# Reading x again and saving the bias: two transfers put at other places among the latent weights of layer 0

## The chip, the core and the metric

The kernel runs on one core of one Trainium2 chip. The metric is the device time of one execution in microseconds. Each kernel is run several times and the median is compared. Engines are called by the profile's short names: PE is TensorE (matmul), PEld its weight loads, DVE is VectorE, ACT is ScalarE, POOL is GpSimd, SP is SyncE, which here only issues transfers.

## The reference

A two-layer bidirectional encoder on 256 tokens of width 2048, all in float32. Each layer has an attention part with two groups of heads side by side, then an MLP of width 8192, and both parts are modulated by a conditioning vector `c`. Cut to what matters:

```python
mod = silu(c) @ w_ada[l] + b_ada[l]          # 6 vectors of 2048 per layer
h = rmsnorm(x) * (1 + sc_a) + sh_a
proj = h @ w_in[l]                           # dq, dk, dv, cq (512), ckv (256), kr (64)
out_a = diff_attention(dq, dk, dv, positions, bias_table, ...)     # 4 heads, two score maps each
q  = rmsnorm(cq,  q_norm_g[l])  @ w_uq[l]    # 8 heads x (128 plain + 64 positional)
kv = rmsnorm(ckv, kv_norm_g[l]) @ w_ukv[l]   # 8 heads x (128 keys + 128 values)
out_b = mla_attention(q_nope, rope(q_rope), k_nope, rope(kr), v_m)
x = x + g_a * (concat(out_a, out_b) @ w_o[l])
x = x + g_m * (relu(h2 @ w_mlp_in[l])**2 @ w_mlp_out[l])           # h2: x normed and modulated again
```

The result is the normed x after both layers.

## The kernel before

**How the work is tiled.** Activations stand transposed, 128 features by 256 tokens in a tile, and weights are streamed through the chip once. A weight tile comes as 128 partitions by 2048 float32 (1 MiB). For the large products the kernel splits each float32 number into a rounded part `hi` and a rest `lo` (`part`, lines 146 to 157): ScalarE copies the raw half tile into `hi` (line 151), VectorE subtracts to get `lo` (line 154), and TensorE makes three products per pair, hi with the activation's hi (line 194), hi with its lo (line 197) and lo with its hi (line 198); for value weights these are lines 296 to 298. So before TensorE can use a weight, it must have landed, ScalarE must have rounded both halves, and VectorE must have subtracted twice.

**Buffers.** Raw weight tiles rotate through five buffers named `raw`, the `hi` and `lo` halves through four each. The conditioning weights `w_ada` (`ada_load`, `ada_sums`) use the same five raw buffers: VectorE multiplies each such tile by the conditioning vector and sums it (line 380). About one conditioning tile is loaded per weight tile, by a running credit (`more_ada`), so the two streams alternate on SyncE. A transfer is issued when VectorE has freed its buffer.

**What sets the order.** The program is written in one sequence (`layer`, from line 867 on). A scheduler then lists the instructions for each engine, in an order that follows the written one and its own estimate of when inputs are ready; each of ScalarE, VectorE and SyncE works off its list strictly in order. `behind` pins one instruction after another. There is no hand-written table: where a transfer is written changes the scheduler's estimate, and with it the lists of all engines.

**The place.** After the keys of the differential heads come, in the order in which they are written:

- `up_k` (weights `w_uk`, one tile): the latent keys, eight tiles `pss`, copied as `kn`
- `probs(3)`: scores `psc` of the last differential head (line 1249), score minima (1251), exponentials on ScalarE (1236), and the combination on VectorE (1257, 1260, 1261)
- a copy of the attention bias to DRAM (line 981, `bias_kept`), since its buffer is later overwritten by the gate rows and layer 1 needs it again, and a second reading of the input x in token-major form (line 983, two transfers of 1 MiB into `self.xr`), which the residual updates need much later (lines 1117 and 1119). Both happen in layer 0 alone
- `up_q(0)`: plain queries of heads 0 to 3 (weights `w_uq[0, 0]`, 48 matmuls), copied as `qn`
- `turn(0)`: four transposes `pt` of the first head's probabilities (line 1268), copied as `aT` by ScalarE
- `up_r`: positional queries (weights `w_uq[0, 2]`, 48 matmuls), copied as `qr`, then rotated: a permutation matmul `pqr` (line 1222) and VectorE's lines 1225 to 1227
- `turn(1)`, the scores of the first latent head (`psm`, lines 1318 and 1319), `up_v`: the latent values (weights `w_uv`, `pv`, copied as `vm`)
- `turn(2)`, two more steps of latent heads, `up_q(1)`: plain queries of heads 4 to 7 (weights `w_uq[0, 1]`), and then the value projection with the remaining latent heads in between, and the output projection with the residual updates

All copies out of PSUM named here are line 346 on ScalarE.

Of the kernel before, what the change touches and what calls it, by code (L numbers as in the profile page):

```python
# [101 lines left out]
class Trunk:  # L102
# [764 lines left out]
    def layer(self, l, acc=None):  # L867
        nc, io = self.nc, self.io
# [52 lines left out]
        def up_q(b):  # L921
            qn.extend(self.copy(ps, "qn", ms) for ps in self.small(io["w_uq"][l, b], cq, 4))

        def up_r():
            raw = [self.copy(ps, "qr", ms) for ps in self.small(io["w_uq"][l, 2], cq, 4)]
            qr.extend(self.rope_q(x) for x in raw)

        def up_v():
            w = self.weights(io["w_uv"][l])
            for cg in range(2):  # L930
                pss = [self.bank("pv") for _ in range(2)]
                self.tokens_by_k(pss, [[z[:, 512 * cg : 512 * cg + 512] for z in y] for y in w], ckv, True, True)
                vm.append([self.copy(ps, "vm") for ps in pss])
# [12 lines left out]
        def probs(hd):  # L946
            return lambda: a.append(self.diff_probs(l, hd, q[hd], kk[hd]))

        def turn(hd):
            return lambda: at.append(self.transposed(a[hd]))  # L950
# [26 lines left out]
            self.rate = RATE_A2  # L977
        up_k()
        probs(3)()
        if l == 0:  # L980
            nc.sync.dma_start(self.bias_kept, self.row)
            for t in range(2):
                nc.sync.dma_start(self.xr[:, t], io["x"][t])
        up_q(0)
        turn(0)()
        up_r()
        turn(1)()
        mla[0]()
        up_v()
        turn(2)()  # L990
        for f in mla[1:3]:
            f()
# [441 lines left out]
```

## Time and profile before

| What | us |
|---|---|
| median of 3 runs | 2174.59 |
| lowest and highest | 2174.57, 2177.94 |
| the profiled execution: its own time | 2174.76 |
| its span, first to last instruction | 2172.8 |
| TensorE busy | 2144.7 |
| VectorE busy | 1590.9 |
| ScalarE busy | 1139.8 |

Times in rows of the profile count from the start of the span. In the order of time a row gives start, duration, engine, line, operation, tile written and tiles read, shape, count, and in brackets the idle time of the engine before it with what ended it. The groups of waits give the waiting line, the one that it waited for, total, times and the longest. In the stretches, the granted clock is the share of TensorE's full clock, and the DMA share is the mean busy share of the core's 16 DMA engines.

### The profile page before, as it was taken

How to read it: one execution, taken by the hardware profiler on the slowest of the kernel's cores; microseconds unless marked ns; L12 is line 12 of the kernel's file. 1: busy time of each engine (PE TensorE's matmuls, PEld its weight loads, DVE VectorE, ACT ScalarE, POOL GpSimd, SP SyncE). 2: the span in 40 equal slices, each digit the busy share in tenths (PEclk: the TensorE clock that was granted, in tenths of full speed). 3: DMA queues.
4: the chain of work that ended last, by engine and by line, in shares of the span. 5: the costliest groups of instructions: out<-in, count | busy, mean ns of one | idle time of the engine just before them, and what ended most of it. 6: DMA issues, size and time to landing. Idle time of an engine off the chain costs nothing.

```text
span 2172.8 us, 29358 instructions
## 1 busy us (share of the span) xinstructions
PE 2144.7 (99%) x11502; PEld 1863.5 (86%) x11502; DVE 1590.9 (73%) x2117; ACT 1139.8 (52%) x1725; POOL 6.8 (0%) x19
## 2 busy tenths in 40 slices
PE   7999999999999999999999999999999999999998
PEld 6899888898888888888889998888888888888886
DVE  7888888988688988888876876678555555555555
ACT  6555663565455355355454565556535534644643
POOL 0000000000000000000000000000000000000000
PEclk8999999999999999999999999999999999999999
DMA  9988889799888988888967766767655555565552
GB/s 387 423 340 330 320 328 357 290 330 344 314 329 326 352 315 320 321 333 320 336 224 278 253 229 224 290 214 273 233 199 182 200 194 177 192 208 179 194 195 96
DMA packets 87243, 594.76 MB, mean 274 GB/s; under 512 B 9856, under 2 KB 10304, under 8 KB 20288
## 3 DMA queue, kind: packets, MB, share of 16 engines
q1 hardware_dynamic: 85968, 587.08, 73.5%
q0 software_dynamic: 848, 5.28, 0.6%
q8 instruction: 90, 1.47, 0.3%
q10 hardware_dynamic: 288, 0.52, 0.1%
q14 instruction: 49, 0.40, 0.1%
HBM read 589.66 MB, written 3.18 MB: 273 GB/s over the span
## 4 chain that ended last, share of the span: by engine, by line
PE 97%; DVE 2%; DMA 1%; ACT 0%; SPq 0%; issue 0%; ACTq 0%
PE ps L217 19%; PE pr L312 13%; PE pr L311 13%; PE pr L314 13%; PE ps L220 10%; PE pk L260 3%; PE pk L284 2%; PE pk L194 2%; PE pk L198 2%; PE pk L197 2%; PE pv L298 2%; PE pv L296 2%; PE pv L297 2%; PE pk L281 1%; PE ps L198 1%; PE ps L197 1%
## 5 line engine op out<-in xcount | busy, mean ns | idle before, releaser
L154 DVE TENSOR_TENSOR lo<-raw,hi 128x1024 fp32r<-128x1024 f32 (+1 forms) x714 | 836.0, 1194 | 446.2 <-issue 215.5
L151 ACT ACTIVATE hi<-raw 128x1024 fp32r<-128x1024 f32 (+1 forms) x714 | 732.5, 1036 | 694.0 <-PE pr L312 375.9
L380 DVE SCALAR_TENSOR_TENSOR ada<-ada,cond 128x2048 f32<-128x2048 f32 x192 | 438.0, 2285 | 12.0 <-DMA ada<-in_w_ada 11.4
L217 PE MATMUL ps<-h,hi 128*128 128x512 f32 x1856 | 431.5, 390 | 0.0
L217 PEld LDWEIGHTS ps<-h,hi 128*128 128x128 f32 x1856 | 345.2, 188 | 69.4
L311 PE MATMUL pr<-hi,hid 128*128 128x512 f32 x1024 | 398.6, 389 | 0.0
L312 PE MATMUL pr<-hi,hid 128*128 128x512 f32 x1024 | 398.5, 389 | 0.0
L314 PE MATMUL pr<-lo,hid 128*128 128x512 f32 x1024 | 253.5, 389 | 0.0
L220 PEld LDWEIGHTS ps<-h,lo 128*128 128x128 f32 x1856 | 230.3, 192 | 4.5
L220 PE MATMUL ps<-h,lo 128*128 128x256 f32 x1856 | 231.7, 283 | 0.0
L314 PEld LDWEIGHTS pr<-lo,hid 128*128 128x128 f32 x1024 | 192.2, 188 | 39.9
L312 PEld LDWEIGHTS pr<-hi,hid 128*128 128x128 f32 x1024 | 192.3, 188 | 39.7
L311 PEld LDWEIGHTS pr<-hi,hid 128*128 128x128 f32 x1024 | 192.2, 188 | 39.6
L1192 ACT ACTIVATE sum<-ps 128x256 f32<-128x256 f32 x110 | 42.1, 382 | 117.8 <-PE ps L220 117.7
L194 PE MATMUL pk<-h,hi 128*128 128x256 f32 x320 | 90.5, 285 | 0.2 <-ACT h L705 0.2
L198 PE MATMUL pk<-h,lo 128*128 128x256 f32 x320 | 90.5, 283 | 0.0
L197 PE MATMUL pk<-h,hi 128*128 128x256 f32 x320 | 90.5, 283 | 0.0
L260 PE MATMUL pk<-hf,w 128*128 128x256 f32 x384 | 84.1, 379 | 0.5 <-ACT hf L677 0.5
L188 DVE TENSOR_TENSOR hid<-relu,hid 128x256 fp32r<-128x256 f32 x128 | 48.3, 421 | 49.5 <-ACT hid L187 49.5
L260 PEld LDWEIGHTS pk<-hf,w 128*128 128x128 f32 x384 | 72.7, 190 | 10.7 <-ACT hf L677 0.9
L194 PEld LDWEIGHTS pk<-h,hi 128*128 128x128 f32 x320 | 61.1, 192 | 0.6 <-ACT h L705 0.5
L198 PEld LDWEIGHTS pk<-h,lo 128*128 128x128 f32 x320 | 61.3, 192 | 0.2 <-DVE lo L154 0.2
(237 smaller groups left out, 2456.1 us busy)
## 6 DMA issues: line engine op xcount, KB each, us to landing
raw<-in_w_m SPq DMA_DIRECT2D x238, 1024.0 KB, 5.2
ada<-in_w_ada SPq DMA_DIRECT2D x192, 1024.0 KB, 6.5
raw<-in_w_o SPq DMA_DIRECT2D x32, 1024.0 KB, 6.0
raw<-in_w_m SPq DMA_DIRECT2D x24, 768.0 KB, 5.7
raw<-in_w_dv SPq DMA_DIRECT2D x16, 1024.0 KB, 5.5
raw<-in_w_t SPq DMA_DIRECT2D x12, 1024.0 KB, 5.2
w<-in_w_a SPq DMA_DIRECT2D x24, 384.0 KB, 13.5
raw<-in_w_a SPq DMA_DIRECT2D x12, 768.0 KB, 5.4
```

Source lines behind the costliest of these rows:

```text
L151: ins = self.nc.scalar.activation(hi, v, AF.Copy)
L154: ins = self.nc.vector.tensor_tensor(lo, v, hi.bitcast(F32), ALU.subtract)
L194: ins = mm(ps, hi, x[0], start=first, stop=False, skip_group_check=shared)
L197: mm(ps, hi, x[1], start=False, stop=False, skip_group_check=shared)
L198: self.last_mac = mm(ps, lo, x[0], start=False, stop=last, skip_group_check=shared)
L217: mm(ps.rearrange("p a b -> p (a b)"), part(w, k, 0), x[2], start=k == 0, stop=False)
L220: mm(ps[:, 0], part(w, k, 1), x[0], start=False, stop=k == nk - 1)
L260: self.nc.tensor.matmul(ps, v, whole[k], start=first, stop=last, skip_group_check=True)
L311: mm(ps, xh[:, c], part(i, 0), start=kq == 0 and i == 0, stop=False)
L312: mm(ps, xl[:, c], part(i, 0), start=False, stop=False)
L314: self.last_mm = mm(ps, xh[:, c], part(i, 1), start=False, stop=kq == 3 and i == 3)
L380: ins = nc.vector.scalar_tensor_tensor(w, w, 1.0, self.cond, ALU.mult, ALU.mult, accum_out=acc[:, i : i + 1])
```

## The change

The bias copy and the first half of the second reading of x are written after `up_r`, that is behind the loads of the first plain queries' and the positional queries' weights. The second half of x is written after `up_v`, behind the load of the latent values' weights. Before, all three were written ahead of `up_q(0)`. Nothing else is edited; what is computed stays the same.

```diff
         up_k()
         probs(3)()
-        if l == 0:
-            nc.sync.dma_start(self.bias_kept, self.row)
-            for t in range(2):
-                nc.sync.dma_start(self.xr[:, t], io["x"][t])
         up_q(0)
         turn(0)()
         up_r()
+        if l == 0:
+            nc.sync.dma_start(self.bias_kept, self.row)
+            nc.sync.dma_start(self.xr[:, 0], io["x"][0])
         turn(1)()
         mla[0]()
         up_v()
+        if l == 0:
+            nc.sync.dma_start(self.xr[:, 1], io["x"][1])
         turn(2)()
```

Lines below the edit stand one further down in the changed kernel (1236 becomes 1237, and so on), and some tiles have other numbers.

SyncE's list at the moved reads, from the conditioning tile behind `w_uk` on (ada is a tile of conditioning weights, raw a tile of weights; w_uq comes three times, for the first plain, the positional and the remaining plain queries). Before:

```order
L364 DMA ada_1833<-in_w_ada 128x2048
L983 DMA x<-in_x 128x2048 x2
L170 DMA raw_1929<-in_w_uq 128x2048
L364 DMA ada_1940<-in_w_ada 128x2048
L364 DMA ada_1942<-in_w_ada 128x2048
L170 DMA raw_2005<-in_w_uq 128x2048
L364 DMA ada_2018<-in_w_ada 128x2048
L170 DMA raw_2109<-in_w_uv 128x2048
L364 DMA ada_2121<-in_w_ada 128x2048
L170 DMA raw_2189<-in_w_uq 128x2048
```

And in the changed kernel:

```order
L364 DMA ada_1833<-in_w_ada 128x2048
L170 DMA raw_1926<-in_w_uq 128x2048
L364 DMA ada_1937<-in_w_ada 128x2048
L364 DMA ada_1939<-in_w_ada 128x2048
L170 DMA raw_2002<-in_w_uq 128x2048
L364 DMA ada_2015<-in_w_ada 128x2048
L985 DMA x<-in_x 128x2048
L170 DMA raw_2108<-in_w_uv 128x2048
L364 DMA ada_2120<-in_w_ada 128x2048
L990 DMA x<-in_x 128x2048
L170 DMA raw_2189<-in_w_uq 128x2048
```

The two reads of x went behind five and seven other transfers. The bias copy does not show here: the scheduler puts it further up, between two tiles of `w_t`, and it stands there in both kernels.

ScalarE's list at the latent queries (kn, k, qn, qr are copies of products; s are the exponentials of the last differential head; aT is the copy of transposed probabilities; hi is a rounded half of the raw tile named). Before:

```order
L346 ACTIVATE kn_1893<-pss_1880 128x512
L151 ACTIVATE hi_1931<-raw_1929 128x1024
L1236 ACTIVATE s_1896,tot_1902<-s_1896,mx_1897 128x256 x2
L151 ACTIVATE hi_1935<-raw_1929 128x1024
L1236 ACTIVATE s_1908,tot_1914<-s_1908,mx_1909 128x256 x2
L346 ACTIVATE qn_1969<-pss_1944 128x512
L346 ACTIVATE qn_1996<-pss_1971 128x512
L346 ACTIVATE aT_2003<-pt_1998 128x512
L151 ACTIVATE hi_2007<-raw_2005 128x1024
L151 ACTIVATE hi_2011<-raw_2005 128x1024
L346 ACTIVATE qr_2045<-pss_2020 128x512
```

And in the changed kernel, from the last exponentials of the head before on:

```order
L1237 ACTIVATE s_1740,tot_1746<-s_1740,mx_1741 128x256 x2
L151 ACTIVATE hi_1928<-raw_1926 128x1024
L151 ACTIVATE hi_1932<-raw_1926 128x1024
L346 ACTIVATE k_1819<-ps_1664 128x512
L346 ACTIVATE kn_1848<-pss_1835 128x512
L346 ACTIVATE kn_1863<-pss_1850 128x512
L346 ACTIVATE kn_1878<-pss_1865 128x512
L346 ACTIVATE kn_1893<-pss_1880 128x512
L1237 ACTIVATE s_1896,tot_1902<-s_1896,mx_1897 128x256 x2
L1237 ACTIVATE s_1908,tot_1914<-s_1908,mx_1909 128x256 x2
L151 ACTIVATE hi_2004<-raw_2002 128x1024
L151 ACTIVATE hi_2008<-raw_2002 128x1024
```

The rounds of the first queries' weights moved ahead of the last key's copy and of the four latent key copies, and those of the positional queries' weights moved ahead of the query copies. On VectorE the rests of the first queries' weights moved up too, ahead of the combination of the head before, and one conditioning sum (of ada_1833) moved ahead of the last head's score minima; it had stood behind them.

ScalarE's list further on, at the latent values (vm are copies of value tiles, sm the exponentials or the scaling of a latent head, raw_2189 the weights of the remaining plain queries). Before:

```order
L346 ACTIVATE aT_2091<-pt_2086 128x512
L151 ACTIVATE hi_2191<-raw_2189 128x1024
L151 ACTIVATE hi_2195<-raw_2189 128x1024
L1236 ACTIVATE sm_2094,tot_2102<-sm_2094,mxm_2095 128x256 x2
L346 ACTIVATE vm_2137<-pv_2123 128x512
L346 ACTIVATE vm_2139<-pv_2124 128x512
L346 ACTIVATE vm_2155<-pv_2141 128x512
L1324 ACTIVATE sm_2094<-sm_2094,r_2103 128x256 x2
L346 ACTIVATE vm_2157<-pv_2142 128x512
L346 ACTIVATE aT_2164<-pt_2159 128x512
```

And in the changed kernel:

```order
L346 ACTIVATE aT_2090<-pt_2085 128x512
L346 ACTIVATE vm_2136<-pv_2122 128x512
L1237 ACTIVATE sm_2093,tot_2101<-sm_2093,mxm_2094 128x256 x2
L346 ACTIVATE vm_2138<-pv_2123 128x512
L346 ACTIVATE vm_2154<-pv_2140 128x512
L151 ACTIVATE hi_2191<-raw_2189 128x1024
L1325 ACTIVATE sm_2093<-sm_2093,r_2102 128x256 x2
L346 ACTIVATE vm_2156<-pv_2141 128x512
L346 ACTIVATE aT_2164<-pt_2159 128x512
L151 ACTIVATE hi_2195<-raw_2189 128x1024
```

The two rounds of the remaining queries' weights moved behind the value copies and the next transpose's copy. From there to the end of layer 0's output projection ScalarE's and VectorE's lists differ by neighbours that change places, TensorE's in a few such places; after that, and in all of layer 1, the lists are the same.

## Prediction

> **What bounds the kernel now.** I read the page first, then stretches of 10 us around the moved lines, then who made TensorE wait there, then the order of time on each engine.
>
> ```profile
> PE 2144.7 (99%) x11502; PEld 1863.5 (86%) x11502; DVE 1590.9 (73%) x2117; ACT 1139.8 (52%) x1725; POOL 6.8 (0%) x19
> ```
>
> TensorE is busy for 2144.7 of 2172.8 us, so only some 28 us of the span are not matmul at all. An edit to DMA issues can gain only where TensorE waits or runs at a lower clock. The stretches show one such place beside the moved lines. Columns: stretch, length, busy time of PE, PEld, DVE, ACT and POOL, granted clock, DMA share, GB/s.
>
> ```profile
> 190.00:200.00 10.00, 10.00 (x80) 9.79 (x79) 8.74 (x23) 4.59 (x12) 0.00 (x0) 1.00 1.01 424
> 200.00:210.00 10.00, 9.74 (x72) 8.83 (x71) 6.53 (x16) 5.77 (x14) 0.00 (x0) 1.00 0.58 222
> 210.00:220.00 10.00, 7.36 (x41) 6.95 (x40) 7.61 (x9) 3.14 (x5) 0.00 (x0) 0.71 0.73 278
> 220.00:230.00 10.00, 10.00 (x52) 7.99 (x52) 7.67 (x16) 6.29 (x10) 0.00 (x0) 0.95 0.64 221
> 214.80:221.60 6.80, 6.77 (x34) 6.78 (x35) 5.60 (x6) 0.82 (x2) 0.00 (x0) 0.54 0.70 259
> ```
>
> From 210 to 220 TensorE idles 2.64 us, and from 214.8 to 221.6 it is granted 0.54 of its clock; just before, the DMA engines are full (424 GB/s), and in the stall they are not. The waits of TensorE from 200 to 224 (total, times, longest) and its rows in order of time:
>
> ```profile
> PE pss L194 <- ACT hi L151: 2.1, 1, 2.1
> PE pss L198 <- DVE lo L154: 0.7, 2, 0.5
> ...
> 191.77 1.89 PE L1249 MATMUL psc<-k,q 128*128 128x256 f32 x8
> 193.31 0.47 PE L197 MATMUL ps<-h,hi 128*128 128x256 f32 x1
> ...
> 202.37 1.89 PE L1249 MATMUL psc<-k,q 128*128 128x256 f32 x8
> 213.57 0.39 PE L194 MATMUL pss<-lath,hi 128*128 128x256 f32 x1 [2.12 <-ACT hi L151]
> 214.83 0.58 PE L198 MATMUL pss<-lath,lo 128*128 128x256 f32 x1 [0.52 <-DVE lo L154]
> 222.90 2.03 PE L1222 MATMUL pqr<-qr,K 128*128 128x512 f32 x4
> 234.97 0.36 PE L194 MATMUL pss<-lath,hi 128*128 128x256 f32 x1
> 240.81 0.60 PE L1268 MATMUL pt<-ident,a 128*128 128x128 f32 x4
> 241.25 0.38 PE L1318 MATMUL psm<-kn,qn 128*128 128x256 f32 x1
> ```
>
> The wait at 213.57 is for the rounded half `hi` of the positional queries' weights (`w_uq[0, 2]`, called raw_2005 in the order), the one at 214.83 for its rest `lo`. Whether ScalarE was late there because of the DMA or because of its own order, the next rows tell: SyncE's issues, the time from issue to landing of the two query transfers (least, median, most), the DMA rate from 189 to 203, and ScalarE.
>
> ```profile
> 184.43 1.26 SPq L983 DMA_DIRECT2D x<-in_x  x2
> 187.15 0.33 SPq L170 DMA_DIRECT2D raw<-in_w_uq  x1
> 197.74 0.33 SPq L170 DMA_DIRECT2D raw<-in_w_uq  x1
> DMA to landing us min/median/max: 9.0/10.3/11.6
> 189.00:203.00 14.00, 14.00 (x110) 13.73 (x109) 9.70 (x27) 6.91 (x16) 0.00 (x0) 1.00 1.01 424
> ...
> 196.16 0.19 ACT L1236 ACTIVATION_READ_ACCUMULATOR s<-s,mx 128x1 f32 x1
> 203.06 1.05 ACT L151 ACTIVATE hi<-raw 128x1024 fp32r<-128x1024 f32 x1
> 206.84 0.19 ACT L1236 ACTIVATION_READ_ACCUMULATOR s<-s,mx 128x1 f32 x1
> 212.46 2.01 ACT L151 ACTIVATE hi<-raw 128x1024 fp32r<-128x1024 f32 x2
> ```
>
> The first query weights land at 187.15 + 11.6 = 198.8, yet ScalarE rounds them only at 203.06; the positional ones land at 197.74 + 9.0 = 206.7 and are rounded at 212.46. So in the profiled run the data are there 4 to 6 us early, and what holds them is their place in ScalarE's row: behind the copies of the keys and of the queries, which wait for TensorE. TensorE waits for ScalarE, and ScalarE waits for TensorE's earlier tiles.
>
> **The change part by part.** The bias copy keeps its row on SyncE (between two column weights, well ahead of all this), so its move costs and gains nothing. What moves is the two reads of x, 2 x 1 MiB, on one queue. Both had gone ahead of the first query weights; now one goes behind the positional queries' weights, one behind the values' weights. At 424 GB/s the 2.1 MB ahead of the first query weights took 4.9 us, so these land at about 193.8, and the positional ones by about 203. The larger effect is the new order of ScalarE: both weights are rounded one group of rows earlier.
>
> *What goes.* From the scores at 202.37 to the rotation matmul at 222.90 TensorE takes 20.53 us. Its work there at full clock, from undisturbed stretches: scores 193.31 - 191.77 = 1.54; 48 matmuls of one query weight 240.81 - 234.97 = 5.84, twice; four transposes 241.25 - 240.81 = 0.44. Together 13.66, so 6.87 us are waits and lower clock: 2.12 + 0.52 of waits, 6.80 x (1 - 0.54) = 3.1 of clock, and 1.1 of short waits for the first query weights' parts.
>
> *What may come at the first place.* VectorE's rows here and its durations:
>
> ```profile
> 195.42 2.29 DVE L380 SCALAR_TENSOR_TENSOR ada<-ada,cond 128x2048 f32<-128x2048 f32 x1
> 197.83 0.23 DVE L1257 TENSOR_SCALAR c<-r,lam 128x2 f32<-128x2 f32 x1
> 198.09 0.62 DVE L1260 TENSOR_SCALAR s<-s,c 128x256 f32<-128x256 f32 x2
> 198.62 0.88 DVE L1261 SCALAR_TENSOR_TENSOR a<-s,r,s 128x256 f32<-128x256 f32 x2
> 203.44 0.42 DVE L1251 CUSTOM_DVE_ANT_0 s<-psc,bias 128x256 f32<-128x256 f32 x1 [3.94 <-PE psc L1249]
> 213.55 2.36 DVE L154 TENSOR_TENSOR lo<-raw,hi 128x1024 fp32r<-128x1024 f32 x2 [2.40 <-ACT hi L151]
> ```
>
> ScalarE is free at 196.35, rounds the first query weights (2.01) until 198.4, and copies the last key (about 0.6) by 199, in time for the scores at 202.37. VectorE is free at 197.7: 2.36 for the lo parts, 0.23 + 0.62 + 0.88 for the probabilities, and, newly put ahead of the next scores, one conditioning sum of 2.29; together 6.4, until 204.1 (starts follow each other a little closer than these durations). So the score minima start at about 204.0 instead of 203.44. From there to the end of the second exponentials the row took 207.03 - 203.44 = 3.6 with two rounds in between, so 207.2 to 207.6 now; then ScalarE rounds the positional weights until 209.2 to 209.6, and VectorE does 0.23 + 0.62 + 0.88 and the lo parts, until 211.3 to 212. TensorE, without waits, starts those 48 matmuls at 202.37 + 1.54 + 5.84 + 0.44 = 210.2 and needs the second lo part eight matmuls (0.96) later, at 211.15. The wait is between 0.1 and 1.1; I take 0.3, since VectorE's starts are closer than its durations.
>
> *At the second place*, the remaining queries' weights (`w_uq[0, 1]`, raw_2189). Their rounds used to stand right behind a transpose's copy, far ahead; now the second stands behind the value copies and the next transpose's copy. ScalarE's rows before:
>
> ```profile
> 232.46 0.90 ACT L1324 ACTIVATE sm<-sm,r 128x256 f32<-128x256 f32 x2
> 233.26 0.58 ACT L346 ACTIVATE vm<-pv 128x512 f32<-128x512 f32 x1
> 233.73 0.59 ACT L346 ACTIVATE aT<-pt 128x512 f32<-128x512 f32 x1
> ```
>
> In before's time that copy ends at 234.3, the round behind it (1.05) at 235.4, and at 236.4 if the first round, now also in this stretch, pushes it by its full length. TensorE starts this weight at 234.97 and needs the second half 0.96 later, at 235.93, its lo part some 1.3 after that (eight matmuls and three transposes of about 0.12). The wait lies between 0 and 1.0 (the lo part is 1.2 behind the round); I take 0.3.
>
> *Nothing else is paid.* The residual updates that read x, a round of the output projection with its wait, and the waits of ScalarE and of TensorE in that projection:
>
> ```profile
> L1119 DVE TENSOR_TENSOR x<-x,yg x72: 681/685/693, 340.1 to 2165.2; 128x512 f32<-128x512 f32 x72
> 351.40 2.02 ACT L151 ACTIVATE hi<-raw 128x1024 fp32r<-128x1024 f32 x2 [3.36 <-PE pr L312]
> ACT hi L151 <- DMA raw<-in_w_o: 11.7, 3, 5.6
> PE pr L311 <- ACT hi L151: 0.7, 2, 0.4
> ```
>
> The moved reads of x land by about 225 at the latest (issue near 212 plus 11.6), and their first reader comes at 340.1. Whether the gain lives to the end is decided where ScalarE waits for weights, in the output projection. At 351.40 a round waits 3.36 us for TensorE to free its buffer. There the weights are ahead of TensorE as far as buffers let them, so all that follows is set from TensorE's time and moves with it; the later 0.7 us of TensorE's waits stays.
>
> The sum: 6.87 - 0.3 - 0.3 = 6.3 us. The profiled execution took 2174.76 us with a span of 2172.8 (1.96 lie around it) and is 0.17 above the median of 2174.59; 2174.6 - 6.3 gives 2168.3 us.
>
> **Rivals.** *Half the prize stays away (2171.4 to 2172.9 us).* The clock falls although the long wait is gone. If both new waits take their upper bounds and a drop as long as the old one follows, 6.87 - 2.1 - 3.1 leaves 1.7, that is 2172.9; if the old drop is not the waits' doing and comes anyway, 6.87 - 3.1 - 0.6 = 3.2, that is 2171.4. For it: two new waits are tight. Against it: the drop began where 2.64 us of waits lay within 3.4 us (211.45 to 214.83), and the new waits are far apart. The Trainium skill bears on this, "TensorE: Matmul & The Clock Gate", "Why this matters for your kernels": it says that the clock falls back after idle gaps of over about 3 us between bursts. By that rule the old gap of 2.12 us was too short to cost clock, and the change would gain only the waits, 2171.4. The trace disagrees so far as one run can: 0.54 was granted directly behind waits of 2.64 us in all, and 1.00 before and after.
>
> *Given back later (2174.6 us).* The rounds at the output projection wait 11.7 us for DMA, and if transfers, not buffers, set the pace there, an earlier TensorE only waits longer. For it: those 11.7 us. Against it: the wait of 3.36 on TensorE at 351.40, between the two places.
>
> *Slower (about 2180 us).* The second MiB of x now goes directly ahead of the remaining queries' weights. These take the buffer of a conditioning sum that ends at about 213.6 and are issued there; ScalarE's turn for them is at about 225.5 and TensorE can bear 227, so a landing of up to 13.6 us is hidden. The worst landing quoted is 11.6. Beyond 13.6 each us is a wait, beyond about 2.6 us of wait the clock's 3.1 comes on top, and from a landing of 21 us the kernel is slower; at 22 us it is 8.4 + 3.1 - 6.3 = 5.2 above before.
>
> That the change doesn't do what it says is true of the bias copy alone, which is in the forecast.
>
> **How the numbers follow.** The forecast has 0.76, half the prize 0.12, given back 0.06, slower 0.06. A difference of 0.2% (4.3 us) is about what a measurement of this kernel can tell from none. The forecast's own gain runs from 4.8 (both waits at their bounds) to 6.9, and to 7.6 if the 0.7 us at the output projection goes too: all faster, 0.76. Half the prize and given back are within 0.2%, 0.18. The range reaches from 2166.9 to 2172.9, which takes in the first two cases.
>
> **What would show it.** In the profile after: the group of waits of `pss` for `hi` gone or under 0.5 us, the granted clock at 1.00 from 200 to 230, the rotation matmul at about 216.2 instead of 222.9, the weights of the remaining queries' tile with a wait under 1 us, and the distance from there to the end unchanged. A clock of 0.54 near 210 to 220 would make the prediction wrong by the first rival; a longer wait for `hi` after 375 by the second; a wait for `raw` of the query weights in ScalarE's row near 225 by the third.

## The result and the profile after

The changed kernel takes 2171.38 us (median of 20 runs, 2169.66 to 2174.25). The kernel before took 2174.70 us beside it (20 runs, 2172.34 to 2177.94). The ratio is 0.9986 with a 95% interval of 0.998 to 0.9993: a gain of 3.3 us (1.5 to 4.3 by the interval), where 6.3 were forecast. The profiled execution took 2172.34 us with a span of 2170.6.

The stall that the prediction was about is gone. The stretches around the moved lines, in the changed kernel (columns as before):

```profile
200.00:210.00 10.00, 10.00 (x79) 9.79 (x78) 8.17 (x25) 6.16 (x15) 0.00 (x0) 1.00 1.01 397
210.00:220.00 10.00, 10.00 (x74) 8.75 (x73) 9.63 (x13) 5.06 (x8) 0.00 (x0) 1.00 0.72 278
220.00:230.00 10.00, 10.00 (x52) 8.47 (x51) 8.34 (x17) 6.03 (x14) 0.00 (x0) 1.00 0.97 369
```

TensorE is busy throughout, at the full clock. The same places in the order of time: TensorE's scores and its rotation matmul, then ScalarE's rounds of the first queries' and of the positional weights, then VectorE's rest of the latter.

```profile
203.84 1.89 PE L1250 MATMUL psc<-k,q 128*128 128x256 f32 x8
...
217.62 1.97 PE L1223 MATMUL pqr<-qr,K 128*128 128x512 f32 x4
...
197.72 1.99 ACT L151 ACTIVATE hi<-raw 128x1024 fp32r<-128x1024 f32 x2
...
208.40 1.99 ACT L151 ACTIVATE hi<-raw 128x1024 fp32r<-128x1024 f32 x2
...
210.32 2.35 DVE L154 TENSOR_TENSOR lo<-raw,hi 128x1024 fp32r<-128x1024 f32 x2
```

From the scores to the rotation matmul TensorE needs 217.62 - 203.84 = 13.78 us; it needed 20.53. All of this profile runs late, for a reason outside the change, as the next table shows: it gives the start of TensorE's n-th matmul in the two traces. TensorE issues the same count of matmuls in both, and between the last key columns and the output projection only neighbours change places.

| matmul | place | before, us | after, us | earlier by |
|---|---|---|---|---|
| 60 | start | 23.04 | 24.34 | -1.30 |
| 1080 | last key columns | 196.86 | 198.32 | -1.46 |
| 1260 | behind the rotation matmul | 229.25 | 223.92 | 5.33 |
| 1320 | remaining queries | 238.66 | 233.65 | 5.01 |
| 1860 | output projection, layer 0 | 353.17 | 347.93 | 5.24 |
| 1920 | output projection | 366.77 | 362.78 | 3.99 |
| 1980 | output projection | 380.92 | 378.14 | 2.78 |
| 2040 | output projection, end | 395.29 | 393.05 | 2.24 |
| 11460 | end of layer 1 | 2154.79 | 2152.55 | 2.24 |

The start took 1.46 us longer in this one execution. It is not the change's doing: there the two kernels issue the same, and among the other profiles below, whose code is also the same up to there, the 60th matmul starts between 22.73 and 24.76. From 1080 to 1320 TensorE then gains 5.01 + 1.46 = 6.5 us, close to the 6.3 forecast. And from 1860 to 2040 it loses 3.0 of them again. TensorE's waits from 195 to 400 in the changed kernel:

```profile
PE pr L311 <- ACT hi L151: 3.4, 3, 1.4
...
359.71 0.50 PE L311 MATMUL pr<-hi,mo 128*128 128x512 f32 x1 [0.96 <-ACT hi L151]
372.32 0.50 PE L311 MATMUL pr<-hi,do 128*128 128x512 f32 x1 [1.44 <-ACT hi L151]
384.53 0.50 PE L311 MATMUL pr<-hi,mo 128*128 128x512 f32 x1 [0.99 <-ACT hi L151]
```

No wait is left but these three, where before had 0.7 us in two. Why `hi` was late there, ScalarE's rows say, those of the changed kernel. TensorE's three waits ended with the rounds that start at 358.61, 371.21 and 383.44:

```profile
348.25 2.01 ACT L151 ACTIVATE hi<-raw 128x1024 fp32r<-128x1024 f32 x2 [3.20 <-DMA raw<-in_w_o]
...
358.61 1.99 ACT L151 ACTIVATE hi<-raw 128x1024 fp32r<-128x1024 f32 x2
363.36 2.01 ACT L151 ACTIVATE hi<-raw 128x1024 fp32r<-128x1024 f32 x2 [2.75 <-DMA raw<-in_w_o]
371.21 2.01 ACT L151 ACTIVATE hi<-raw 128x1024 fp32r<-128x1024 f32 x2 [5.84 <-DVE mod L394]
...
383.44 1.99 ACT L151 ACTIVATE hi<-raw 128x1024 fp32r<-128x1024 f32 x2
```

Only the middle one waited for its weights: their transfer was issued at 364.28 and landed 6.8 us later, at 371.1. (The row names VectorE's `mod`, which ran from 371.06 to 371.22 and is not among what the round reads.) The weights of the other two were issued at 348.73 and 374.69 and landed after 7.5 and 7.0 us, that is 2.4 and 1.7 us before they were rounded. What held these two is ScalarE's list once more: squares of the new x stand ahead of them (L1134), and these wait for VectorE. At the first of the two VectorE's list had changed. Its rows in the changed kernel, then in the kernel before (`yg` reads TensorE's output, `x` is the updated x):

```profile
353.12 0.69 DVE L1118 TENSOR_TENSOR yg<-pr,bias 128x512 f32<-128x512 f32 x1 [1.41 <-PE pr L314]
353.73 2.28 DVE L380 SCALAR_TENSOR_TENSOR ada<-ada,cond 128x2048 f32<-128x2048 f32 x1
355.93 0.69 DVE L1120 TENSOR_TENSOR x<-x,yg 128x512 f32<-128x512 f32 x1
```

```profile
358.35 0.69 DVE L1117 TENSOR_TENSOR yg<-pr,bias 128x512 f32<-128x512 f32 x1 [0.43 <-PE pr L314]
359.08 0.69 DVE L1119 TENSOR_TENSOR x<-x,yg 128x512 f32<-128x512 f32 x1
```

`yg` comes 5.23 us earlier, in step with TensorE. Behind it stands a conditioning sum now, which before stood ahead of it, and so `x`, the squares and the round come only 3.15 us earlier. At this place TensorE's 5.24 us became 3.98, at the late landing they became 2.22, and the third place cost nothing net, since the kernel before waits near it too (0.28 us at 380.58 and 0.41 at 386.76).

The round at 348.25 is the one that started at 351.40 before and waited 3.36 us for TensorE to free its buffer. Now it waits 3.20 us for its DMA: it comes only 3.15 us earlier, while TensorE is 5.24 earlier there. So a lead of the weights over TensorE was being used up. ScalarE's rounds in the value projection show the same drift: the second round of one value tile ran at 242.09 before and at 242.03 now, though TensorE came 5 us earlier. The rows, of before and then of after:

```profile
242.09 1.06 ACT L151 ACTIVATE hi<-raw 128x1024 fp32r<-128x1024 f32 x1
```

```profile
242.03 1.05 ACT L151 ACTIVATE hi<-raw 128x1024 fp32r<-128x1024 f32 x1
```

That gave the theory for the experiments, which leaves out the place in VectorE's list that the rows above show. **Theory:** the stall was ScalarE's order, as forecast; what the change gains there is in part given back in layer 0's output projection, because the weights come at a pace of their own, in company with the conditioning stream (L364 and L380: 1 MiB transfers on SyncE that share the five `raw` buffers with the weights, and 2.3 us of VectorE each). **Rivals:** the stall was the landing of the weights behind 2 MiB of x; and what was lost later came of something else than that stream.

### The profile page after: what moved, and what is told of

It is laid out like the page before. It is cut to its first block, busy times and chain, and to the rows that moved or that the text cites. A ratio compares the mean times of both kernels' runs of the same rounds, so it can differ in the third digit from the quotient of the medians.

```text
span 2170.6 us, 29350 instructions
## 1 busy us (share of the span) xinstructions
PE 2142.9 (99%) x11502; PEld 1862.3 (86%) x11502; DVE 1591.3 (73%) x2117; ACT 1140.3 (53%) x1725; POOL 6.8 (0%) x19
## 4 chain that ended last, share of the span: by engine, by line
PE 96%; DVE 2%; DMA 1%; ACT 1%; issue 0%; SPq 0%; ACTq 0%; DVEq 0%
PE ps L217 19%; PE pr L311 13%; PE pr L312 13%; PE pr L314 13%; PE ps L220 10%; PE pk L260 3%; PE pk L284 2%; PE pk L194 2%; PE pk L198 2%; PE pk L197 2%; PE pv L298 2%; PE pv L296 2%; PE pv L297 2%; PE pk L281 1%; PE ps L198 1%; PE ps L197 1%
## 5 line engine op out<-in xcount | busy, mean ns | idle before, releaser
L380 DVE SCALAR_TENSOR_TENSOR ada<-ada,cond 128x2048 f32<-128x2048 f32 x192 | 438.1, 2285 | 11.9 <-DMA ada<-in_w_ada 11.4
```

Of the source, the lines that this page charges most:

```text
L380: ins = nc.vector.scalar_tensor_tensor(w, w, 1.0, self.cond, ALU.mult, ALU.mult, accum_out=acc[:, i : i + 1])
```

## Experiments

Each was timed in interleaved runs with the kernel before; its median in these sessions was 2174.4 to 2175.25 us. The ratio is always to that kernel's runs of the same session.

### 1. ScalarE's rounds put back

```diff
-    def small(self, src, xs, n):
+    def small(self, src, xs, n, pin=False):
...
-        w = self.weights(src)
+        w = self.weights(src, order=(self.last_copy, None) if pin else None)
...
-            raw = [self.copy(ps, "qr", ms) for ps in self.small(io["w_uq"][l, 2], cq, 4)]
+            raw = [self.copy(ps, "qr", ms) for ps in self.small(io["w_uq"][l, 2], cq, 4, l == 0)]
```

(`last_copy` is the last copy that was written, the last key's or the transpose's; the first queries are pinned in the same way.)

> The changed kernel, with ScalarE's rounds of the first and of the positional query weights pinned back behind the last key copy and the transpose's copy; the reads of x stay behind the weights on SyncE. Theory (ScalarE's order held the weights): TensorE waits again some 2 us for the positional hi and the clock drops behind it, so the whole time returns to 2173.5 to 2175 us. Rival (the landing of the weights behind 2 MiB of x held them): the weights still land earlier, the waits stay away, and the time stays at 2170.5 to 2172 us.

Measured: 2174.23 us, ratio 0.9996 (0.9988 to 1.0005). The gain is gone. TensorE's waits and the stretch around it:

```profile
PE pss L194 <- ACT hi L151: 2.1, 1, 2.1
PE pss L198 <- DVE lo L154: 0.7, 2, 0.5
...
210.00:220.00 10.00, 7.36 (x49) 6.95 (x48) 7.57 (x12) 5.58 (x7) 0.00 (x0) 0.83 0.94 360
...
198.73 0.33 SPq L170 DMA_DIRECT2D raw<-in_w_uq  x1
199.11 0.43 SPq L985 DMA_DIRECT2D x<-in_x  x1
...
213.46 2.00 ACT L151 ACTIVATE hi<-raw 128x1024 fp32r<-128x1024 f32 x2
```

The reads of x still stand behind the positional weights on SyncE here (198.73, then 199.11). ScalarE rounds those weights at 213.46, with no wait in front of it, and TensorE waits its 2.1 us as before. The landing is not what held TensorE; the places in the lists are. VectorE's list went back with ScalarE's, though the edit pins ScalarE alone: the conditioning sum that the change had put ahead of the last head's score minima stands behind them again (208.28, the minima between 204.43 and 207.1). So this run doesn't tell the two engines apart.

### 2. ScalarE's rounds moved, the reads of x left ahead

```diff
+PRE_K, PRE_Q = 0, 0
...
+        def reads():
+            nc.sync.dma_start(self.bias_kept, self.row)
+            for t in range(2):
+                nc.sync.dma_start(self.xr[:, t], io["x"][t])
...
+            for n, ps in enumerate(self.small(io["w_uk"][l], ckv, 8)):
+                if l == 0 and n == PRE_K:
+                    reads()
+                    self.pre[0] = self.weights(io["w_uq"][l, 0])
+                kn.append(self.copy(ps, "kn"))
+                if l == 0 and n == PRE_K:
+                    self.behind(self.last_copy, self.last_hi)
```

(The same is done for the positional weights ahead of the first query copy. SyncE's list is before's, word for word.)

> The kernel before, its reads of x still ahead of the first query weights on SyncE, with only ScalarE's rounds moved: those of w_uq[0,0] ahead of the key copies, those of w_uq[0,2] ahead of the query copies; VectorE's and TensorE's lists stay as before but for a row or two. Theory (ScalarE's place is the cause, and the data landed early enough): the 2.1 us wait for hi of the positional weights goes, 0 to 1 us of waits for lo stay, and the time is 2171 to 2173 us. Rival (both are needed: the weights behind 2 MiB of x land at 198.8, the rounds then hold up the key copies and TensorE's banks): a wait for the key copies or for hi of the first query weights of 1 to 3 us takes its place, and the time is 2174 to 2176 us.

Measured: 2172.82 us, ratio 0.9992 (0.9983 to 1.0). That is half the way. TensorE's waits from 200 to 216 in order of time, then ScalarE's two pairs of rounds, then VectorE between them:

```profile
205.76 0.39 PE L200 MATMUL pss<-lath,lo 128*128 128x256 f32 x1 [0.23 <-DVE lo L156]
211.65 0.39 PE L196 MATMUL pss<-lath,hi 128*128 128x256 f32 x1 [0.35 <-ACT hi L153]
213.74 0.58 PE L200 MATMUL pss<-lath,lo 128*128 128x256 f32 x1 [1.35 <-DVE lo L156]
...
199.24 2.01 ACT L153 ACTIVATE hi<-raw 128x1024 fp32r<-128x1024 f32 x2 [1.48 <-DMA raw<-in_w_uq]
...
210.56 1.99 ACT L153 ACTIVATE hi<-raw 128x1024 fp32r<-128x1024 f32 x2
...
206.76 2.28 DVE L382 SCALAR_TENSOR_TENSOR ada<-ada,cond 128x2048 f32<-128x2048 f32 x1
...
209.04 0.40 DVE L1265 CUSTOM_DVE_ANT_0 s<-psc,bias 128x256 f32<-128x256 f32 x1
...
212.47 2.35 DVE L156 TENSOR_TENSOR lo<-raw,hi 128x1024 fp32r<-128x1024 f32 x2
```

The wait for `hi` fell from 2.1 to 0.35 us, but `lo` of the positional weights is 1.35 late (1.6 us of waits for `lo` in all, where 0 to 1 were expected). Behind 2 MiB of x ScalarE waits 1.48 us for the first weights; TensorE has no wait from that until 205.76, so my rival did not happen as it was put. What is late is VectorE. Its list is neither that of before nor that of the changed kernel: a conditioning sum (206.76) stands between the two pairs of score minima, ahead of the second (209.04); behind those come the exponentials, and only then the rounds (210.56) and the rests (212.47). In the kernel before that sum stands behind both pairs (207.29), in the changed kernel ahead of both (202.95), and there the rounds start at 208.40 - 1.46 = 206.9 by before's time. So the new places of ScalarE's rounds bring part of the gain while the reads of x stay where they were. How much of the rest is VectorE's order isn't shown: no kernel here moves one engine's list and leaves the other's. From matmul 1080 to 1260 this profile gains 2.5 us (at a clock of 0.94 from 205 to 235), where the changed kernel's gained 6.8.

### 3 and 4. The conditioning stream left out of the output projection

```diff
+        self.lean = l == 0
         self.gate(l, 2)
...
+        l, g, i = self.ada_todo.pop(0)
+        if self.lean:
+            self.ada_here.append((None, l, g, i))
+            return
...
+            if w is None:
+                ins = nc.vector.memset(acc[:, i : i + 1], 0.0)
```

> The changed kernel without the conditioning stream in layer 0's output projection: the 15 transfers issued there and their sums on VectorE are left out (their part of the modulation counts as zero). Theory A (weights came late there because the stream shares SyncE, the five buffers and VectorE with them, and that gave back 3.0 of the 6.5 us): no wait of TensorE from 310 to 400, and 2167 to 2169 us, some 6 to 7.5 under the kernel before. Theory B (what was given back came of something else, as of ScalarE's waits for TensorE's buffers): 2170.5 to 2172 us.

> The kernel before, without the stream in the same stretch (the same 15 transfers and sums left out). Theory A: it has only 0.7 us of waits to lose, so 2173.5 to 2175 us, and 5 to 6.5 us above the changed kernel without the stream. Theory B: the distance stays at the 3.3 us that the two kernels showed with the stream.

Measured: the changed kernel 2167.32 us, ratio 0.9964 (0.9952 to 0.9977); the kernel before 2172.97 us, ratio 0.9988 (0.9979 to 0.9997). The distance between the two is 5.65 us without the stream, 3.3 with it. The output projection in the changed kernel with the stream, and then without it:

```profile
340.00:395.00 55.00, 51.61 (x225) 41.76 (x224) 47.66 (x52) 20.76 (x26) 0.00 (x0) 1.00 0.92 342
```

```profile
340.00:395.00 55.00, 55.00 (x244) 45.54 (x243) 30.31 (x46) 23.46 (x32) 0.00 (x0) 1.00 0.47 163
```

51.61 of 55 us became 55.00: the 3.4 us of waits are gone. From matmul 1320 to 2040 the changed kernel took 159.4 us with the stream and the kernel before 156.6; without it they took 154.9 and 154.7 (one profile of each). So the 2.8 us more of the changed kernel come with the stream. The medians alone wouldn't show it: the intervals of the two ratios are 3.9 and 5.4 us wide. Nor does this pair show by which way the stream took the gain back, since without it the lists there are others too: in the changed kernel without the stream ScalarE's round (353.73) stands ahead of the first squares (354.69). The kernel before gained 1.7 us from the same cut, 0.7 of it its waits there.

### 5 and 6. Half of it: transfers halved, or sums halved

In the first pair the transfers of that stretch are halved and each sum runs twice over its half; in the other kernel the transfers are whole and the sums run over a half. Half of these sums' input is left out in all three.

```diff
+        if self.lean:
+            self.nc.sync.dma_start(w[:, : D // 2], src[:, : D // 2])
+        else:
+            self.nc.sync.dma_start(w, src)
```

```diff
+            c = slice(0, D // 2) if self.lean else slice(0, D)
             ins = nc.vector.scalar_tensor_tensor(
-                w, w, 1.0, self.cond, ALU.mult, ALU.mult, accum_out=acc[:, i : i + 1]
+                w[:, c], w[:, c], 1.0, self.cond[:, c], ALU.mult, ALU.mult, accum_out=acc[:, i : i + 1]
             )
```

> The changed kernel, in which the conditioning weights issued during layer 0's output projection load only half their columns; the sum runs over that half twice, so VectorE's time stays. The other half of those sums' input is left out. Theory A (in that projection the transfers set the pace, so 3.0 of the 6.5 us gained at the query weights were given back there): the projection loses its waits, 2167.5 to 2169.5 us, 2 to 4 under the changed kernel. Theory B (buffers or VectorE set the pace there, transfers are not late): 2170.5 to 2172 us, like the changed kernel.

> The kernel before, with the same halved conditioning loads in layer 0's output projection (half of those sums' input left out). Theory A: little to win here, since before's later TensorE waits only 0.7 us for hi there: 2173 to 2174.5 us, and the full 5 to 6.5 us above the halved changed kernel. Theory B: the same time as before, and only 3 us above the halved changed kernel.

> The changed kernel with full conditioning loads, whose sums in layer 0's output projection run over half the columns only (VectorE some 1.1 us less for each; half of those sums' input left out). Theory A (transfers): at most 1 us under the changed kernel, 2170.3 to 2172 us. Theory B (VectorE's time or the buffers it holds): 2 to 4 us under it, 2167.5 to 2169.5 us.

Measured: 2170.69 us (ratio 0.9978, 0.997 to 0.9987) for the changed kernel with half the transfers, 2174.28 us (0.9995, 0.9986 to 1.0004) for the kernel before with them, and 2169.86 us (0.9974, 0.9964 to 0.9984) for the changed kernel with half the sums. Against the expectations, theory A (the transfers set the pace) missed: it asked for 2167.5 to 2169.5 us with half the transfers, where 2170.69 came, and for a distance of 5 to 6.5 us between the pair, where 3.6 came. Half the sums came out between the ranges of the two theories. But all these intervals reach into that of the changed kernel itself, so the times alone don't decide. The stretches from 340 to 395, half the transfers and half the sums:

```profile
340.00:395.00 55.00, 55.00 (x244) 45.56 (x243) 51.10 (x76) 21.49 (x28) 0.00 (x0) 1.00 0.84 291
```

```profile
340.00:395.00 55.00, 54.00 (x236) 43.83 (x235) 38.78 (x53) 21.18 (x27) 0.00 (x0) 1.00 0.91 356
```

Half the sums remove 2.4 of the 3.4 us of waits; the 1.0 that stays is at the third place. With half the transfers no wait is left, but that proves little: TensorE had lost its lead ahead of that, where it waited 1.6 us for a head's output and had a lower clock behind it (two short sums for one long one change VectorE's list; that this is the reason wasn't tried):

```profile
PE pot L1318 <- ACT o L1309: 1.6, 1, 1.6
...
320.00:325.00 5.00, 4.24 (x16) 3.05 (x16) 3.29 (x5) 4.34 (x13) 0.00 (x0) 0.69 0.73 293
```

From matmul 1080 to 1860 this kernel took 153.1 us, the changed kernel 149.6 and the one with half the sums 150.3. So the first came 3.5 us later to the place of the waits and wasn't tested by it. Half the sums bear out that VectorE's sums are part of the cause. Whether the pace of the transfers is another stays open: each is one half of a loop. The transfer that landed late was issued at 364.28, as a conditioning sum ended (361.96 + 2.28 = 364.24), and that sum stands behind the rest `lo` (359.69) of the very round that the first place had held up.

### 7 to 10. The stream moved instead of cut

```diff
+RATE_O, RATE_K = 0.8, 0.9
 FILL = "0|1|2|3||||rlm"
...
+        if l == 0:
+            self.rate = RATE_O
         self.gate(l, 2)
```

(Two others have 0.8 and 0.75, and 0.9 and 0.75. Nothing is left out in these four kernels.)

> The changed kernel with the stream thinned in layer 0's output projection (0.8 transfers for each weight instead of 1.1) and made up in the norm behind it (0.9 instead of 0.6): four transfers and sums move there, everything is computed. Theory A: the waits from 345 to 395 shrink, 2168.5 to 2170.5 us, unless the sums now come late at the norm near 460, which would show as a wait there. Theory B: 2170.5 to 2172.5 us.

> The kernel before with the same two rates. Theory A: at most 0.7 us to win, 2174 to 2175.5 us, and 4 to 6 us above the changed kernel with these rates. Theory B: the distance stays at 3.3 us.

> The changed kernel with 0.8 conditioning transfers for each weight in layer 0's output projection, as in the experiment before, and 0.75 instead of 0.9 in the norm behind it. Theory (the 1.5 us that were lost near 468 in that experiment were weights held up by the denser stream): no wait from 455 to 480 and 2167.5 to 2169 us, unless the sums that the norm needs come late. Rival (the sums then come late): a wait of 1 to 4 us near 460 to 480, 2170 to 2173 us.

> The changed kernel with 0.9 transfers for each weight in the output projection and 0.75 in the norm: two to three transfers move. Theory: most of the 3.0 us of waits from 345 to 395 go, at most 1 us of them stays, nothing is lost near 468: 2168 to 2169.5 us. Rival (late sums): as above, 2170 to 2173 us.

Measured:

| output projection, norm | kernel | us | ratio (95%) |
|---|---|---|---|
| 0.8, 0.9 | changed | 2169.13 | 0.9969 (0.9958 to 0.9981) |
| 0.8, 0.9 | before | 2174.60 | 0.9998 (0.9989 to 1.0007) |
| 0.8, 0.75 | changed | 2169.64 | 0.9975 (0.9965 to 0.9985) |
| 0.9, 0.75 | changed | 2167.87 | 0.9969 (0.9956 to 0.9981) |

The changed kernel gains from the thinner stream, the kernel before doesn't: 5.5 us lie between them now, 3.3 with the old rates. In all three changed kernels TensorE is busy for 55.00 of 55 us from 340 to 395. The rates change the lists there as well: with 0.9 and 0.75 `x` stands right behind `yg` again (`yg` at 351.65, `x` at 352.37). What is left over is paid in the norm, where the stream went. TensorE's waits from 400 to 500 with 0.8 and 0.9, with 0.8 and 0.75, and with 0.9 and 0.75:

```profile
PE pk L195 <- ACT hi L152: 0.6, 1, 0.6
PE pk L195 <- ACT h L706: 0.2, 1, 0.2
```

```profile
PE pk L195 <- ACT h L706: 1.4, 2, 1.1
PE pk L198 <- DVE h L711: 0.5, 1, 0.5
```

```profile
PE ps L218 <- ACT hi L152: 0.8, 1, 0.8
```

The first loses there for late weights, the second for late sums, so there my theory's 2169 at most was missed, by the rival's mechanism and at less than its price: 2169.64. The third beats both kernels, 2167.87 us. Which of the first and the third is better, the intervals don't tell.

## Why the prediction was right and where it failed

**The stall and its cause: right.** The order held the weights, not the landing (experiment 1 brings the stall back with the reads of x left where the change put them), and the data landed early enough to round them early. The forecast laid it to ScalarE's list; VectorE's list changed with it in every run, so ScalarE's part alone isn't shown (experiment 2). ScalarE took up the first weights at 197.72 and ended the positional ones at 210.39, VectorE their rest at 212.67. Less the 1.46 us of the start these are 196.26, 208.9 and 211.2; the prediction had 196.35, 209.2 to 209.6 and 211.3 to 212.

**The new waits: right.** At the first place 13.78 us stand where 13.66 + 0.3 were expected, and the rotation matmul came at 217.62 - 1.46 = 216.16 (216.2 expected). At the second, TensorE lost 5.33 - 5.01 = 0.3 us, as taken. No `raw` of a query weight was waited for near 225, so the third rival did not occur, and nobody waited for the second reading of x or for the saved bias.

**The clock's 3.1 us: mis-sized.** This term came out of one profile. Five profiles now have the same waits there, 2.1 us for `hi` and two for `lo` of 0.7 in all. The clock from 205 to 235, in the kernel before and in the kernel before without the stream:

```profile
205.00:235.00 30.00, 27.10 (x153) 23.48 (x150) 25.24 (x41) 16.16 (x30) 0.00 (x0) 0.89 0.66 238
```

```profile
205.00:235.00 30.00, 27.07 (x173) 23.33 (x172) 27.58 (x47) 18.70 (x35) 0.00 (x0) 1.00 0.75 272
```

It is 0.89 and 1.00. In the kernels with the rounds put back, with half the transfers and with the changed rates (each on before's order of ScalarE):

```profile
205.00:235.00 30.00, 27.11 (x163) 23.39 (x162) 26.61 (x43) 17.91 (x35) 0.00 (x0) 0.94 0.78 279
```

```profile
205.00:235.00 30.00, 27.07 (x170) 23.06 (x169) 27.57 (x45) 18.69 (x36) 0.00 (x0) 1.00 0.71 256
```

```profile
205.00:235.00 30.00, 27.06 (x161) 23.55 (x161) 26.51 (x45) 17.39 (x31) 0.00 (x0) 0.94 0.71 256
```

That is 3.3, 0, 1.8, 0 and 1.8 us of 30, 1.4 on the mean. Where it dropped, the clock stood at 0.50, for 6.8 us in the kernel before (214.2 to 221.0) and for 3.4 us in the two others. In the changed kernel, and in all six others in which the stall is gone whole, it stayed full:

```profile
205.00:235.00 30.00, 29.90 (x202) 26.84 (x201) 25.48 (x50) 19.78 (x41) 0.00 (x0) 1.00 0.81 312
```

So the drop goes with the stall, but follows it in some executions and not in others. The Trainium skill, "TensorE: Matmul & The Clock Gate", "Why this matters for your kernels", names idle gaps of over about 3 us: two of the five profiles agree with that (2.1 us, no drop), three do not. The mean clock that is on record for every execution agrees with the smaller term: it is 0.9957 over 116 executions with the whole stall and 0.9965 over 65 without any of it, that is 9.3 and 7.5 us of lost clock in the whole span, 1.8 apart (standard error 0.4). With 1.4 in place of 3.1 the sum would have been 4.6; the pairs of kernels without the give-back are 5.5 and 5.65 us apart, between the two sums and too rough to choose.

**The step that failed:** "There the weights are ahead of TensorE as far as buffers let them, so all that follows is set from TensorE's time and moves with it; the later 0.7 us of TensorE's waits stays." It rested on one row, the round at 351.40 that waited for TensorE. That row shows that the weights had a lead at that one round, not how long the lead was. The rounds around it waited for DMA, in the kernel before:

```profile
334.94 2.01 ACT L151 ACTIVATE hi<-raw 128x1024 fp32r<-128x1024 f32 x2 [1.76 <-DMA raw<-in_w_o]
...
365.19 2.01 ACT L151 ACTIVATE hi<-raw 128x1024 fp32r<-128x1024 f32 x2 [1.44 <-DMA raw<-in_w_o]
372.76 2.01 ACT L151 ACTIVATE hi<-raw 128x1024 fp32r<-128x1024 f32 x2 [5.56 <-DMA raw<-in_w_o]
379.46 2.01 ACT L151 ACTIVATE hi<-raw 128x1024 fp32r<-128x1024 f32 x2 [4.69 <-DMA raw<-in_w_o]
```

So the lead was short; TensorE, 5.2 us earlier, ran through it, and the waits grew from 0.7 to 3.4 us. The row itself turned into a wait for DMA. And the step took the lists there to be the same, where VectorE's sum had moved between `yg` and `x`: 1.26 of the 3.0 us went at that place, 1.76 at the late landing behind it. My second rival, given back later, had the landing half of this mechanism, and at 0.06 it was priced too low; but it was not all or nothing, as I had it: 3.0 of 6.5 us went. Experiments 3 and 4 show that the stream is needed for the loss, and 7 to 10 that moving it brings most of the gain back; what the list's order does there without the stream, or the stream with the old order, wasn't run.

**The number.** The forecast's own gain of 4.8 to 7.6 us does not contain the measured 3.3 (1.5 to 4.3). The time lies within the stated range only because that range was drawn down to the rivals' prices, which is luck as far as the mechanism goes. Both errors have the same sign: 6.3 less 3.0 given back and less 1.3 to 1.7 of clock is 1.6 to 2.0, inside the measured interval.

**The first rival** (half the prize stays away, 2171.4 to 2172.9) has 2171.4 at its end, the time that was measured, but its mechanism did not occur: the clock stayed at 1.00.

## What to carry to other kernels

A gain at one stall lives only as far as the work behind it can be fed earlier: look, in the stage that follows, for the smallest lead of the weights over the engine, and price the gain at what the lead holds. A single wait "for the buffer" doesn't show a lead; count the waits for DMA around it, and look which rounds stand in their list behind something that waits for another engine. Where a scheduler lists the instructions, compare the lists of every engine in that stage too: an edit that moves one can move the others. And where one profile shows a lower clock, look at a second one before it becomes a term of the sum.

## What the runs showed of the hardware beside that

The same waits, 2.1 us the longest, went with a lower clock in three profiles of five, and a wait of 1.6 us in another place with 0.69 over 5 us (the halved transfers), so the length of a wait alone doesn't settle it. The drop was to 0.50 and lasted 3.4 us or twice that. And the start alone moves the time of a single profile: the 60th matmul began between 22.73 and 24.76 us in kernels that are the same up to there, a spread of 2.0 us, more than half of the difference between the two kernels. Only a table by matmul showed the change through that.
